# Hybrid SSD / S5 / Conformer step on one core: where the SSD output is split, where state work is queued, and how the LayerNorm mean is made

## The chip, the cores and the metric

One core of a Trainium2 chip runs the whole program. The metric is the device time of one launch in microseconds (us); the kernel before takes 1678.6 us, the median of three runs (1676.21 to 1682.48).

## What is computed

Two layers run for a prompt group of 512 tokens and a sample group of 8 x 8 tokens that share all weights; both groups lie side by side as 576 columns, and the 1024 channels are eight tiles of 128 partitions.

```python
# layer 0
xn = rms_norm(x)
proj = xn @ w_in                       # z | x,B,C | dt | u
ya = mamba2(proj[...])                 # 4 groups: y*silu(z), RMSNorm in the group, * norm_w
yb = s5(proj[...])                     # complex diagonal scan, GELU, GLU with w_glu
x = x + concat([ya, yb]) @ w_out
x = x + square(relu(rms_norm(x) @ w_ff1)) @ w_ff2
# layer 1
h = rms_norm(x) @ w_pw1 + b_pw1        # 2048 columns
h = h[:, :1024] * sigmoid(h[:, 1024:])
h, new_buf = causal_depthwise_conv(h, buf, w_dw, b_dw)     # 31 taps for each channel
h = silu(layer_norm(h))                # mean and variance over the 1024 channels
x = x + h @ w_pw2 + b_pw2
x = x + square(relu(rms_norm(x) @ w_ff1)) @ w_ff2
y = rms_norm(x)
```

Beside `y` the new states are outputs: conv buffers, the SSD states (`o_assm`), the S5 states and the depthwise buffers (`o_cconv`).

## The kernel before, in words

Everything is fp32. A matmul of activations and weights is made of three fp32r products (hi·hi, hi·lo, lo·hi). `mm` (L215) does one 128-column block of weights: 8 slices of the contraction x 3 products x 2 halves of 288 columns = 48 matmuls into one PSUM tile. Its weights come through `load` (L203): `raw` by a DMA that SP issues (L208), `hi` by ScalarE (L211), `lo` by VectorE (L212), each in two buffers, so SP, ScalarE and VectorE must each get through one block while TensorE multiplies another.

A scheduler fixes the order on each engine when the program is built; each engine then runs its list in order, and an instruction that waits holds up all behind it. `hp` raises the priority of what is in it; everything else takes the place the scheduler's own estimate gives it, which can be far ahead of where the code stands.

The stages, in us of the profiled span: mixer of layer 0 to about 585 (`mixer0`, the last part of it the w_out product), MLP 0 (`_ffn(0)`) to 1000, Conformer (`conformer`) to 1255, MLP 1 to 1650, final norm to 1672.5. What the change touches:

- **SSD output** (`a_group`, L975 to L988): each of four groups ends with two tiles `ya` scaled by `rg` (L986) and written to DRAM as `yad` (L987). Before the first half of w_out, `reload` (L1120, L1142) reads eight `yad` tiles back (`rl`) and splits them with `split_scaled` into `yah` (ScalarE, L248) and `yal` (VectorE, L249). Each block m of that product reads its `x` from `xrd` (L1146) and adds the PSUM tile to it (L1148).
- **State work** in MLP 0 (`_ffn`, L367 to L377): in each of 8 up/down pairs of q = 0 stands one piece of `ssm_state` (sample update of the SSD state: `bt`, `xw`, `h` in by DMA; `bm`, `xs`, `bs`, `h` on VectorE; `ss` on TensorE, L1022; `o_assm` out, L1025), and in each of q = 1 one piece of `dwconv_state` (`hs` in, `o_cconv` out, products `pr` and sums `ss` on VectorE, L1329 and L1330). They need nothing of the MLP, and the scheduler draws many of them ahead into the w_out stretch.
- **Conformer loop** (L1179 to L1200): two `mm` per m (16 in all), then `hb`, the gated input of the depthwise convolution. A channel tile's 31 taps are done in one of three ways: on TensorE out of order-of-four layouts (`dwconv_pe`, m in `PT`, 36 matmuls `pc<-hq`, L1308), as VectorE multiply-adds (L1376, `ND[m]` of them), or as diagonal fp32r matmuls (`pc<-hh`, L1374, 3 for each tap).
- **LayerNorm**: the mean over channels comes from `tap_sums` (`pt<-hb`, L1259), which is written to DRAM (`pzd`) and read back skewed (`pk`), and from `mu<-pk` (L1282); `nmu` is added to the tiles as they are ready. Squares go to `tsum` (L1216, 80 records), then the reciprocal root, a broadcast (`bc`, `rBl`), the scaling (L1222), Silu (L1223), the split (L256, L258, L259) and the eight blocks of w_pw2 (L1226).

Of the kernel before, what the change touches and what calls it, by code (L numbers as in the profile page):

```python
# [8 lines left out]
F32 = mybir.dt.float32  # L9
# [6 lines left out]
NT = 576  # L16
# [126 lines left out]
class Build:  # L143
# [32 lines left out]
    X2 = 9  # L176
# [24 lines left out]


    def load(self, src, eng=None):  # L203
# [11 lines left out]
    def mm(self, src, act, eng=None, halves=(0, 1)):  # L215
# [5 lines left out]
        for kb in range(8):  # L221
# [104 lines left out]
    def _ffn(self, i, x):  # L326
# [397 lines left out]
    def a_conv_init(self):  # L724
# [15 lines left out]
        self.yad = [self.dp.tile([128, NT], F32, tag="yad%d" % i, name="yad%d" % i) for i in range(8)]  # L740
# [127 lines left out]
    def a_group(self, g, q, X, bank):  # L868
# [174 lines left out]
    def mixer0(self):  # L1043
        nc, I = self.nc, self.I
        with self.tc.tile_pool(name="q1", bufs=5) as self.q1, ExitStack() as inner:
# [43 lines left out]
            q2 = []  # L1089
# [30 lines left out]
            def reload(d, f):  # L1120
                out = []
                for k in range(8):
# [30 lines left out]
    ND = [0, 30, 0, 0, 30, 0, 30, 14]  # L1153

    NEV = 1
    ORD = [0, 1, 2, 3, 4, 5, 6, 7]
# [12 lines left out]
    PT = [0, 2, 3, 5]  # L1169
    NDM = 5  # L1170

    def conformer(self, x):
        nc, I = self.nc, self.I
        with self.tc.tile_pool(name="q2", bufs=2) as q:
# [3 lines left out]
            ps31 = [self.bank("pt0"), self.bank("pt1", "sf")]  # L1178
            for m in range(8):  # L1179
# [3 lines left out]
                nc.scalar.activation(s, s, AF.Sigmoid, bias=self.v("bpw1", 8 + m))  # L1183
                ps = self.mm(I["w_pw1"][m], act)
# [17 lines left out]
            self.dwconv(q, 7, hbs[7], acc[7], nmu)  # L1202
            nmu = nmu[0]

            ts = self.bank("tsum")
            for n, k in enumerate(self.ORD):
                if k < 7:
                    nc.vector.tensor_tensor(acc[k], acc[k], nmu, op=ALU.add)
                s = self.B("sq")
                if self.SQ[n] == "a":  # L1210
                    nc.scalar.activation(s, acc[k], AF.Square)
                else:
                    nc.vector.tensor_tensor(s, acc[k], acc[k], op=ALU.mult)
                for c in (0, 4, 1, 2, 3):
                    m = min(128, NT - c * 128)
                    nc.tensor.matmul(ts[:m, c:c + 1], s[:, c * 128:c * 128 + m], self.ones[:, 0:1], start=n + c == 0, stop=(n, c) == (7, 3))  # L1216
# [3 lines left out]
            act = []  # L1220
            for k in range(8):
                nc.vector.tensor_tensor(acc[k], acc[k], rB, op=ALU.mult)  # L1222
                nc.scalar.activation(acc[k], acc[k], AF.Silu, scale=self.v("lnw", k), bias=self.v("lnb", k))  # L1223
                act.append(self.split(acc[k], "fx", self.B, k == 0))
# [4 lines left out]
    def dwconv_init(self, q):  # L1229
# [7 lines left out]
        self.bdc = q.tile([128, 8], F32, tag="bdc", name="bdc")  # L1237
        self.neg = q.tile([128, 128], F32, tag="neg", name="neg")
        nc.gpsimd.memset(self.neg, -1.0 / 1024)
        self.pzd = self.dp.tile([31, 670], F32, tag="pzd", name="pzd")  # L1240
# [4 lines left out]
    def dwconv_center(self):  # L1245

        nc = self.nc
        s = self.tp.tile([128, NT], F32, tag="sa", name="s1", bufs=1)
        nc.vector.tensor_reduce(s[:, 0:64], self.ss.rearrange("p m t -> p t m"), axis=mybir.AxisListType.X, op=ALU.add)
        nc.vector.tensor_reduce(s[:, 64:65], self.v("bdw", 0, 8), axis=mybir.AxisListType.X, op=ALU.add)  # L1250
        ps = self.bank("cm")
        nc.tensor.matmul(ps[:, 0:65], self.neg, s[:, 0:65], start=True, stop=True)
        nc.vector.tensor_tensor(self.ss, self.ss, ps[:, 0:64].unsqueeze(1).broadcast_to([128, 8, 64]), op=ALU.add)
        nc.vector.tensor_tensor(self.bdc, self.v("bdw", 0, 8), ps[:, 64:65].broadcast_to([128, 8]), op=ALU.add)

    def tap_sums(self, q, m, hb, ps):

        for h in range(2):
            self.nc.tensor.matmul(ps[h][:31, 0:H], self.v("dww", m * 31, 31), hb[:, 30 + h * H:30 + h * H + H], start=m == 0, stop=m == 7)  # L1259

    def neg_mean(self, q, ps):

        nc = self.nc
        pz = q.tile([31, 670], F32, tag="pz", name="pz", bufs=1)
        pk = q.tile([31, NT], F32, tag="pk", name="pk", bufs=1)
        nc.gpsimd.memset(pz[:, 0:30], 0.0)
        nc.gpsimd.memset(pz[:, 542:670], 0.0)
        nc.gpsimd.memset(pk[:, NP:NT], 0.0)
        out = q.tile([128, NT], F32, tag="nmu", name="nmu", bufs=1)
        with self.hp():  # L1270
            nc.scalar.activation(pz[:, 30:30 + H], ps[0][:31, 0:H], AF.Copy)
            nc.scalar.activation(pz[:, 30 + H:542], ps[1][:31, 0:NP - H], AF.Copy)
            nc.scalar.activation(pz[:, 542:670].rearrange("p (b j) -> p b j", b=8)[:, :, 8:16],
                                 ps[1][:31, NP - H:H].rearrange("p (b j) -> p b j", b=8), AF.Copy)
            nc.sync.dma_start(self.pzd, pz)
            nc.scalar.activation(q.tile([31, 1], F32, tag="ld", name="ld", bufs=1), pz[:, 31:32], AF.Silu)
            d = self.pzd
            nc.sync.dma_start(pk[23:31, NP:NT], bass.AP(tensor=d.tensor, offset=d.offset + 23 * 671 + 520, ap=[[671, 8], [16, 8], [1, 8]]))
            nc.sync.dma_start(pk[:, 0:NP], bass.AP(tensor=d.tensor, offset=d.offset, ap=[[671, 31], [1, NP]]))
            mu = self.pm.tile([128, 2, 512], F32, tag="mm", name="mu")[:, :, :H]  # L1280
            for h, o, n in ((0, 0, H), (1, 0, NP - H), (1, NP - H, 64)):
                nc.tensor.matmul(mu[:, h, o:o + n], self.neg[:31], pk[:, h * H + o:h * H + o + n], start=True, stop=True)  # L1282
            nc.scalar.activation(h2(out), mu, AF.Copy)
        return out, pk
# [7 lines left out]
    def dwconv_pe(self, q, m, hb, a):  # L1292
# [18 lines left out]
        with self.hp(self.HPC):  # L1311
# [5 lines left out]
            nc.scalar.activation(a[:, 0:NP].rearrange("p (n f) -> p f n", f=4), y, AF.Identity, bias=self.bdc[:, m:m + 1])  # L1317
# [15 lines left out]
    def dwconv(self, q, m, hb, a, nmu=None):  # L1333
# [9 lines left out]
        if nmu is not None:  # L1343
            nc.vector.tensor_tensor(a[:, NP:], a[:, NP:], nmu[0][:, NP:], op=ALU.add)
# [7 lines left out]
        nc.scalar.activation(ap, hb[:, 0:NP], AF.Identity, scale=w(0), bias=self.bdc[:, m:m + 1])  # L1352
        pc = None
        if k0 < 31:
# [6 lines left out]
            if nmu is not None:  # L1361
                with self.hp(self.HPC):
                    nc.tensor.matmul(pc, self.neg[:31], nmu[1][:, 0:NP], start=True, stop=False)
            for k in range(k0, 31, 4):
# [7 lines left out]
                for j in range(n):  # L1372
                    for i, (dd, h) in enumerate(((dh, hh), (dh, hl), (dl, hh))):
                        nc.tensor.matmul(pc, dd[:, j], h[:, k + j:k + j + NP], start=k + j == k0 and i == 0 and nmu is None, stop=k + j == 30 and i == 2)  # L1374
        for k in range(1, k0):
            nc.vector.scalar_tensor_tensor(ap, hb[:, k:k + NP], w(k), ap, op0=ALU.mult, op1=ALU.add)  # L1376
        if pc is None and nmu is not None:
            nc.vector.tensor_tensor(ap, ap, nmu[0][:, 0:NP], op=ALU.add)
# [40 lines left out]
```

## Time and profile before

| | us |
|---|---|
| three runs, median (lowest, highest) | 1678.6 (1676.21, 1682.48) |
| the profiled execution, its own time | 1674.24 |
| its span | 1672.5 |
| TensorE busy (share of the span) | 1591.3 (95%) |
| VectorE busy | 1054.5 (63%) |
| ScalarE busy | 634.8 (38%) |
| granted TensorE clock, mean | 0.97 of full |

All sums are made within the profiled execution, whose time is 4.4 us under the median. An engine's rows give the start, the busy time and the count of merged records; a matmul of 288 columns is one record, an fp32 one that isn't fp32r is two. In the views of waits and of the timeline "<-" names what ended the idle time.

### The profile page before, as it was taken

What the parts mean: (1) busy time and instruction counts of PE and PEld (TensorE: products, weight loads), DVE (VectorE), ACT (ScalarE), POOL (GpSimd) and SP (SyncE); (2) the same over time, 40 slices, a digit from 0 to 9 for tenths busy, and PEclk for the clock granted to TensorE, in tenths of its full rate; (3) what the DMA queues carried; (4) which work ended last, traced back from release to release, by engine and by line L of the source; (5) the groups of instructions that cost most, each with busy time, mean ns of one, the idle gap of its engine ahead of it and who ended that gap; (6) DMA issues with size and microseconds to landing.
All of it is one profiled execution on the core that took longest, in us unless ns stands there. A gap on an engine that the chain in (4) does not pass through costs nothing.

```text
span 1672.5 us, 28815 instructions
## 1 busy us (share of the span) xinstructions
PE 1591.3 (95%) x11833; PEld 1557.6 (93%) x11833; DVE 1054.5 (63%) x1796; ACT 634.8 (38%) x1081; POOL 4.7 (0%) x45
## 2 busy tenths in 40 slices
PE   7999889999998999999999999996799999999997
PEld 7999789989897999999999999995799999999996
DVE  7988899876647966754443557587454443444466
ACT  4244556675514333322222353223333222222244
POOL 0000000000000000000000000000000000000000
PEclk9999999999998999999999999997799999999998
DMA  6644457687766434432222245641022222222234
GB/s 197 180 109 132 131 172 197 197 267 220 251 234 188 94 97 129 154 127 78 87 77 88 78 146 148 189 107 30 25 77 77 89 76 89 85 81 88 78 127 132
DMA packets 149883, 214.43 MB, mean 128 GB/s; under 512 B 59034, under 2 KB 94874, under 8 KB 149752
## 3 DMA queue, kind: packets, MB, share of 16 engines
q1 hardware_dynamic: 146088, 211.28, 41.2%
q8 instruction: 93, 1.52, 0.4%
q10 hardware_dynamic: 3664, 1.32, 0.3%
q14 instruction: 38, 0.31, 0.1%
HBM read 181.22 MB, written 31.34 MB: 127 GB/s over the span
## 4 chain that ended last, share of the span: by engine, by line
PE 82%; DVE 7%; DMA 6%; ACT 2%; issue 1%; SPq 1%; ACTq 0%; DVEq 0%
PE mm L226 72%; PE pc L1308 2%; DVE lo L212 1%; DMA sg<-cumd 1%; DMA rl<-yad 1%; PE pc L1374 1%; PE tsum L1216 1%; PE bc L310 1%; DMA rl<-ybd 1%; DMA rl<-yg 1%; PE pt L1259 1%; DMA ud<-u 1%; PE s5s L600 1%; PE s5y L704 0%; PE s5y L705 0%
## 5 line engine op out<-in xcount | busy, mean ns | idle before, releaser
L211 ACT ACTIVATE hi<-raw 128x1024 fp32r<-128x1024 f32 x217 | 229.7, 1060 | 740.2 <-PE mm L226 685.6
L226 PE MATMUL mm<-fxh,hi 128*128 128x288 f32 x1920 | 418.2, 299 | 23.8 <-ACT hi L211 10.4
L212 DVE TENSOR_TENSOR lo<-raw,hi 128x1024 fp32r<-128x1024 f32 x217 | 264.8, 1221 | 259.0 <-ACT hi L211 257.5
L226 PE MATMUL mm<-fxh,lo 128*128 128x288 f32 x1920 | 417.4, 298 | 0.0
L226 PE MATMUL mm<-fxl,hi 128*128 128x288 f32 x1920 | 415.0, 298 | 0.0
L226 PEld LDWEIGHTS mm<-fxh,hi 128*128 128x128 f32 x1920 | 311.7, 190 | 26.7 <-ACT hi L211 12.7
L226 PEld LDWEIGHTS mm<-fxh,lo 128*128 128x128 f32 x1920 | 311.6, 190 | 1.8 <-issue 1.1
L226 PEld LDWEIGHTS mm<-fxl,hi 128*128 128x128 f32 x1920 | 311.9, 190 | 0.4
L226 PE MATMUL mm<-gh,hi 128*128 128x288 f32 x1024 | 230.0, 295 | 0.0
L226 PE MATMUL mm<-gh,lo 128*128 128x288 f32 x1024 | 229.4, 295 | 0.5 <-DVE lo L212 0.5
L226 PE MATMUL mm<-gl,hi 128*128 128x288 f32 x1024 | 229.5, 295 | 0.0
L226 PEld LDWEIGHTS mm<-gh,lo 128*128 128x128 f32 x1024 | 167.5, 188 | 0.8 <-DVE lo L212 0.8
L226 PEld LDWEIGHTS mm<-gl,hi 128*128 128x128 f32 x1024 | 167.9, 188 | 0.0
L226 PEld LDWEIGHTS mm<-gh,hi 128*128 128x128 f32 x1024 | 167.6, 188 | 0.0
L350 DVE TENSOR_TENSOR fft<-mm,r2B 128x576 f32<-128x576 f32 x56 | 42.4, 758 | 140.5 <-PE mm L226 140.5
L1376 DVE SCALAR_TENSOR_TENSOR acc<-hb,vec,acc 128x512 f32<-128x512 f32 x104 | 77.2, 748 | 1.3
L343 DVE TENSOR_TENSOR ffr<-ffr 128x576 f32<-128x576 f32 x64 | 48.5, 758 | 2.3 <-ACT gh L342 0.4
L344 DVE TENSOR_TENSOR gl<-ffr,gh 128x576 fp32r<-128x576 f32 x64 | 48.5, 758 | 2.1
L342 ACT ACTIVATE gh<-ffr 128x576 fp32r<-128x576 f32 x64 | 44.1, 689 | 2.0
L351 DVE TENSOR_TENSOR x<-x,fft 128x576 f32<-128x576 f32 x56 | 42.4, 758 | 1.8
L765 DVE SCALAR_TENSOR_TENSOR cvo<-xb,vh,cvo 128x600 f32<-128x600 f32 x48 | 40.0, 833 | 1.4 <-ACT cvo L763 1.4
L340 ACT ACTIVATE ffr<-mm 128x576 f32<-128x576 f32 x64 | 40.6, 634 | 0.0
(356 smaller groups left out, 1903.1 us busy)
## 6 DMA issues: line engine op xcount, KB each, us to landing
raw<-w_ff SPq DMA_DIRECT2D x136, 512.0 KB, 3.5
raw<-w_in SPq DMA_DIRECT2D x33, 512.0 KB, 3.7
raw<-w_pw SPq DMA_DIRECT2D x24, 512.0 KB, 3.6
dm<-dwm SPq DMA_DIRECT2D x16, 576.0 KB, 5.9
h<-ass SPq DMA_DIRECT2D x16, 512.0 KB, 4.7
raw<-w_out SPq DMA_DIRECT2D x16, 512.0 KB, 4.5
U<-ud SPq DMA_DIRECT2D x16, 288.0 KB, 3.0
xsd<-xs SPq DMA_DIRECT2D x16, 288.0 KB, 4.0
```

Of the source, the lines that this page charges most:

```text
L211: nc.scalar.activation(hi, raw, AF.Copy)
L212: eng.tensor_tensor(lo, raw, hi.bitcast(F32), op=ALU.subtract)
L226: nc.tensor.matmul(ps[:, h, :H], w[:, k], a[:, h * H:(h + 1) * H], start=n == 0, stop=n == 23)
L340: nc.scalar.activation(h2(r), ps, AF.Relu)
L342: nc.scalar.activation(hi, r, AF.Square)
L343: nc.vector.tensor_tensor(r, r, r, op=ALU.mult)
L344: nc.vector.tensor_tensor(lo, r, hi.bitcast(F32), op=ALU.subtract)
L350: nc.vector.tensor_tensor(h2(t), ps, rB, op=ALU.mult)
L351: nc.vector.tensor_tensor(x[m], x[m], t, op=ALU.add)
L765: nc.vector.scalar_tensor_tensor(o[:, 0:600], xb[:, k:k + 600], self.half("acw", 16 * k + m), o[:, 0:600], op0=ALU.mult, op1=ALU.add)
L1308: nc.tensor.matmul(pc[:, g * 128:g * 128 + 128], w[:, j * 128:j * 128 + 128], hq[:, g, j:j + 128], start=j == 0, stop=j == 8)
L1376: nc.vector.scalar_tensor_tensor(ap, hb[:, k:k + NP], w(k), ap, op0=ALU.mult, op1=ALU.add)
```

## The change

1. The two `ya` tiles of groups 1 to 3 are split where they lie, as soon as `rg` is applied, into twelve tiles `yx`; only group 0 goes through DRAM. The w_out product takes the slices in the order 2 to 7, 0, 1. The pool in which `yx` lies gives one buffer (`X2` 9 to 8).
2. `behind_load` lets the pieces of state work issue only after the three instructions of the weight load before them. `dwconv_center` is gone.
3. The mean comes from 16 fp32 matmuls `mu<-acc` that add up in two PSUM banks as the tiles get ready; `tap_sums` and `neg_mean` are gone. `PT` and `ND` are others. After the mean come eight adds on VectorE, squares on ScalarE, four sums of two squares on VectorE, and half as many `tsum` matmuls. `chain` fixes the order on VectorE and ScalarE.

```diff
@@ load @@
-            nc.sync.dma_start(raw, src)
-            nc.scalar.activation(hi, raw, AF.Copy)
-            eng.tensor_tensor(lo, raw, hi.bitcast(F32), op=ALU.subtract)
+            self.last = [nc.sync.dma_start(raw, src), nc.scalar.activation(hi, raw, AF.Copy),
+                         eng.tensor_tensor(lo, raw, hi.bitcast(F32), op=ALU.subtract)]
@@ new @@
+    def chain(self, ins):
+        for a, b in zip(ins, ins[1:]):
+            self.tc.add_manual_dep(b.ins, a.ins.name, mybir.DependencyInfo(mybir.DependencyClass.NoSync, mybir.DependencyReason.DATA),
+                                   reason="chain")
+    def behind_load(self):
+        with ExitStack() as st:
+            for i in self.last:
+                st.enter_context(self.tc.issue_after(i.ins))
+            yield
@@ _ffn @@
                 if q == 1 and i == 0:
-                    self.dwconv_state(self.qp, m)
-                    if m == 7:
-                        self.dwconv_center()
+                    with self.behind_load():
+                        self.dwconv_state(self.qp, m)
                 if q == 0 and i == 0:
-                    self.ssm_state(self.qp, m)
+                    with self.behind_load():
+                        self.ssm_state(self.qp, m)
@@ a_group @@
             nc.vector.tensor_tensor(ya[j], ya[j], rB, op=ALU.mult)
-            nc.sync.dma_start(self.yad[2 * g + j], ya[j])
+            if g:
+                self.ya[2 * g + j] = self.split_scaled(ya[j], self.v("anorm", 2 * g + j), "ya",
+                                                       lambda n, dt: self.yp[0].tile([128, NT], dt, tag="yx", name=n, bufs=12))
+            else:
+                nc.sync.dma_start(self.yad[j], ya[j])
@@ mixer0 @@
+            act += [self.ya[k] for k in range(2, 8)]
...
-                ps = self.mm(I["w_out"][m], act)
+                ps = self.mm(I["w_out"][m], act, order=(2, 3, 4, 5, 6, 7, 0, 1))
@@ conformer @@
-    ND = [0, 30, 0, 0, 30, 0, 30, 14]
+    ND = [0, 30, 0, 30, 0, 30, 0, 20]
-    PT = [0, 2, 3, 5]
+    PT = [0, 2, 4, 6]
...
-                with self.hp(self.HP if m == 7 else 0):
-                    self.tap_sums(q, m, hb, ps31)
                 if m > 0:
                     self.dwconv(q, m - 1, hbs[m - 1], acc[m - 1])
-            nmu = self.neg_mean(q, ps31)
+                if m > 1 and m - 2 not in self.PT:
+                    self.mean(mu, acc, m - 2, done)
+                if m > 3 and m - 4 in self.PT:
+                    self.mean(mu, acc, m - 4, done)
+            self.dwconv(q, 7, hbs[7], acc[7])
+            for m in self.ORD:
+                if m not in done:
+                    self.mean(mu, acc, m, done)
+            for h in range(2):
+                nc.scalar.activation(nmu[:, h * H:h * H + H], mu[h][:, 0:H], AF.Copy)
...
+            for n, k in enumerate(self.ORD):
+                dve.append(nc.vector.tensor_tensor(acc[k], acc[k], nmu, op=ALU.add))
+                sq.append(self.B("sq"))
+                nc.scalar.activation(sq[n], acc[k], AF.Square)
+                if n in (2, 4, 6):
+                    pair(n - 2)
+            pair(6)
+            self.chain(dve)
...
+            for k in range(9):
+                if k < 8:
+                    dve.append(nc.vector.tensor_tensor(acc[k], acc[k], rB, op=ALU.mult))
+                    sca.append(nc.scalar.activation(acc[k], acc[k], AF.Silu, scale=self.v("lnw", k), bias=self.v("lnb", k)))
+                    act.append((self.B("fxh", F32R), self.B("fxl", F32R)))
+                    sca.append(nc.scalar.activation(act[k][0], acc[k], AF.Copy))
+                if k:
+                    dve.append(nc.vector.tensor_tensor(act[k - 1][1], acc[k - 1], act[k - 1][0].bitcast(F32), op=ALU.subtract))
+            self.chain(dve)
+            self.chain(sca)
@@ mean @@
+        for h in range(2):
+            self.nc.tensor.matmul(mu[h][:, 0:H], self.neg, acc[m][:, h * H:h * H + H], start=not done, stop=len(done) == 7)
```

Three places show how the instructions move. First SP's list around the reloads of the SSD output; `raw<-w_out` are the weights of the w_out product, `xr` and `xrd` its x. Before:

```order
L1124 DMA rl<-yad_413 128x576
L1146 DMA x_6506<-xrd_352 128x576
L1003 DMA h_7305<-ass 128x1024
L1323 DMA hs<-ccs 128x8x30
L999 DMA bt_7589<-btd_396 64x128
L1124 DMA rl<-yad_414 128x576
L1139 DMA xrd_353<-xr 128x576
L208 DMA raw<-w_out 128x1024
L1124 DMA rl<-yad_415 128x576
L1324 DMA o_cconv<-hs 128x8x22
L1000 DMA xw_7590<-xwd_400 64x256
L1124 DMA rl<-yad_416 128x576
```

And with the change, from the first reload on:

```order
L1142 DMA rl<-yad_411 128x576
L1165 DMA x_6424<-xrd_351 128x576
L1157 DMA xrd_352<-xr 128x576
L1142 DMA rl<-yad_412 128x576
L224 DMA raw<-w_out 128x1024
L1165 DMA x_6482<-xrd_352 128x576
L1157 DMA xrd_353<-xr 128x576
L224 DMA raw<-w_out 128x1024
L1165 DMA x_6540<-xrd_353 128x576
L224 DMA raw<-w_out 128x1024 x4
L224 DMA raw<-w_ff_0 128x1024 x9
```

Eight reloads are two, and no `h`, `hs`, `bt`, `xw`, `o_cconv` stands among the weights of w_out any more; the first of them come behind nine blocks of MLP 0.

Second, TensorE at the end of the Conformer loop; `mm<-fxh` is the last block of w_pw1. Before:

```order
L226 MATMUL mm<-fxh,lo 128x288 x2
L1259 MATMUL pt_10964<-hb,vec 31x288
L1259 MATMUL pt_10965<-hb,vec 31x288
L1282 MATMUL mu<-pk,neg 128x288
L1282 MATMUL mu<-pk,neg 128x224
L1282 MATMUL mu<-pk,neg 128x64
L1363 MATMUL pc<-pk,neg 128x512
L1374 MATMUL pc<-hh,dh 128x512
```

With the change:

```order
L239 MATMUL mm<-fxh,lo 128x288 x2
L1310 MATMUL pc<-hq,dm 128x128 x36
L1285 MATMUL mu_10931<-acc,neg 128x288
L1285 MATMUL mu_10932<-acc,neg 128x288
L1371 MATMUL pc<-hh,dh 128x512
L1371 MATMUL pc<-hl,dh 128x512
L1371 MATMUL pc<-hh,dl 128x512
```

The skewed reload is gone from the way to the mean; the last `pc<-hq` (m = 6) has moved behind the last block, and three pairs `mu<-acc` stand behind the 30 `pc<-hh`.

Third, VectorE in MLP 0 at the first pair of q = 0; `ffr` and `gl` belong to the up block before, `lo` to the weights. With the change:

```order
L225 TENSOR_TENSOR lo<-raw,hi 128x1024
L1024 TENSOR_TENSOR bm<-bt_7275,cst 32x512
L1035 TENSOR_TENSOR h_7279<-h_7279,cds 128x1024
L1033 TENSOR_TENSOR xs<-xw_7276,xs 32x256
L356 TENSOR_TENSOR ffr<-ffr 128x576
L1029 TENSOR_TENSOR bs<-bm,bs 32x512
L357 TENSOR_TENSOR gl<-ffr,gh 128x576
L225 TENSOR_TENSOR lo<-raw,hi 128x1024
L356 TENSOR_TENSOR ffr<-ffr 128x576
L357 TENSOR_TENSOR gl<-ffr,gh 128x576
L1041 TENSOR_TENSOR h_7279<-h_7279,ss 128x512 x2
L225 TENSOR_TENSOR lo<-raw,hi 128x1024
```

The first piece, which before stood in the w_out stretch, now stands here, and its last step stands in front of a `lo`.

## Rows read from the trace of the kernel before

**Rows 1.** The page, part 4: shares of the chain that ended last, by engine.

```profile
PE 82%; DVE 7%; DMA 6%; ACT 2%; issue 1%; SPq 1%; ACTq 0%; DVEq 0%
```

**Rows 2.** Waits of PE over the span: us in total, times, longest.

```profile
PE mu L1282 <- DMA pk<-pzd: 10.7, 1, 10.7
...
PE mm L226 <- DVE fxh L256: 6.2, 1, 6.2
...
PE mm L226 <- ACT yah L248: 2.6, 3, 1.2
...
PE mm L226 <- DVE yal L249: 2.4, 2, 2.1
```

**Rows 3.** Busy time by stretch: PE, PEld, DVE, ACT, POOL, clock, DMA share, GB/s.

```profile
506.94:585.38 78.44, 70.10 (x479) 67.51 (x477) 69.89 (x83) 29.50 (x40) 0.93 (x6) 0.93 0.58 142
...
535.00:600.00 65.00, 65.00 (x478) 64.78 (x477) 60.16 (x79) 21.94 (x28) 0.93 (x6) 0.98 0.49 110
650.00:727.00 77.00, 77.00 (x583) 77.00 (x582) 53.69 (x69) 29.87 (x44) 0.00 (x0) 1.00 0.48 157
...
1000.00:1135.20 135.20, 135.20 (x1024) 128.59 (x1023) 102.28 (x187) 38.81 (x44) 0.42 (x4) 1.00 0.49 142
...
1135.20:1192.80 57.60, 34.95 (x151) 28.37 (x150) 34.40 (x69) 18.85 (x34) 0.00 (x0) 0.65 0.05 14
```

**Rows 4.** Chain of waits, 490 to 700: start, us, what.

```profile
518.48 5.73 DMA o_assm<-h
...
646.93 0.47 PE ss L1022 x4
647.40 12.78 PE mm L226 x96
```

**Rows 5.** Timeline of PE in the w_out product: start, us, what.

```profile
521.80 0.69 PE L226 MATMUL mm<-yah,hi 128*128 128x288 f32 x2
```

**Rows 6.** Timeline of DVE behind groups 0 and 1.

```profile
429.67 1.23 DVE L212 TENSOR_TENSOR lo<-raw,hi 128x1024 fp32r<-128x1024 f32 x1 [4.35 <-ACT hi L211]
```

**Rows 7.** Groups of PE in the Conformer loop, 1000 to 1135.2: busy, mean ns | idle.

```profile
L1308 PE MATMUL pc<-hq,dm 128*128 128x128 f32 x288 | 33.6, 276 | 0.0
L1259 PE MATMUL pt<-hb,vec 128*31 128x288 f32 x28 | 8.1, 411 | 0.0
```

**Rows 8.** Group of DVE in the same stretch: the multiply-adds.

```profile
L1376 DVE SCALAR_TENSOR_TENSOR acc<-hb,vec,acc 128x512 f32<-128x512 f32 x80 | 59.9, 748 | 1.2
```

**Rows 9.** Chain of waits, 1120 to 1260.

```profile
1138.62 1.84 PE pt L1259 x4
...
1140.96 5.51 DMA pzd<-pz
...
1146.83 4.21 DMA pk<-pzd
...
1168.58 13.03 PE tsum L1216 x80
...
1186.97 5.44 DVE acc L1222 x8
...
1192.83 61.51 PE mm L226 x446
```

**Rows 10.** Timeline of DVE behind the last block of w_pw1.

```profile
1137.76 0.81 DVE L1189 SCALAR_TENSOR_TENSOR hb<-ct,vec,cs 128x576 f32<-128x576 f32 x1
...
1155.07 3.43 DVE L1208 TENSOR_TENSOR acc<-acc,nmu 128x576 f32<-128x576 f32 x5
...
1162.68 4.68 DVE L1376 SCALAR_TENSOR_TENSOR acc<-hb,vec,acc 128x512 f32<-128x512 f32 x6
```

**Rows 11.** Timeline of ACT in the same stretch.

```profile
1153.57 0.65 ACT L1283 ACTIVATE nmu<-mu 128x576 f32<-128x576 f32 x1 [11.11 <-PE mu L1282]
...
1187.76 6.18 ACT L1223 ACTIVATE acc<-acc,vec 128x576 f32<-128x576 f32 x8 [0.83 <-DVE acc L1222]
1193.85 2.39 ACT L258 ACTIVATE fxh<-acc 128x576 fp32r<-128x576 f32 x4
```

More of the change, by code (lines that the diff above doesn't have):

```diff
@@ L1 @@
-from contextlib import ExitStack
+from contextlib import ExitStack, contextmanager
 import numpy as np
@@ L175 @@
     GL = 4
-    X2 = 9
+    X2 = 8
     HPS = 54
@@ L220, in mm @@
         n = 0
-        for kb in range(8):
+        for kb in order:
             ah, al = act[kb]
@@ L739, in a_conv_init @@
         self.ybd = [self.dp.tile([128, NT], F32, tag="ybd%d" % i, name="ybd%d" % i) for i in range(8)]
-        self.yad = [self.dp.tile([128, NT], F32, tag="yad%d" % i, name="yad%d" % i) for i in range(8)]
+        self.yad = [self.dp.tile([128, NT], F32, tag="yad%d" % i, name="yad%d" % i) for i in range(2)]
     def half(self, n, i=0):
@@ L1088, in mixer0 @@
             ssd = [[], []]
-            q2 = []
+            q2 = self.yp = []
+            self.ya = {}
             def side(na):
@@ L1121, in reload @@
                 out = []
-                for k in range(8):
+                for k in range(len(d)):
                     t = self.t("rl", "t")
@@ L1183, in conformer @@
                 nc.scalar.activation(s, s, AF.Sigmoid, bias=self.v("bpw1", 8 + m))
+                if m == 7:
+                    nc.scalar.activation(q.tile([128, 1], F32, tag="ld", name="ld", bufs=1), s[:, 0:1], AF.Silu)
                 ps = self.mm(I["w_pw1"][m], act)
@@ L1196, in conformer, with pair @@
                         self.dwconv_mat(q, m, g)
-                with self.hp(self.HP if m == 7 else 0):
-                    self.tap_sums(q, m, hb, ps31)
                 if m > 0:
                     self.dwconv(q, m - 1, hbs[m - 1], acc[m - 1])
-            nmu = self.neg_mean(q, ps31)
-            self.dwconv(q, 7, hbs[7], acc[7], nmu)
-            nmu = nmu[0]
-            ts = self.bank("tsum")
[L1206 to L1213, printed above, removed]
+                if m > 1 and m - 2 not in self.PT:
[6 more added lines that the diff above has]
+                    self.mean(mu, acc, m, done)
+            nmu = q.tile([128, NT], F32, tag="nmu", name="nmu", bufs=1)
+            for h in range(2):
+                nc.scalar.activation(nmu[:, h * H:h * H + H], mu[h][:, 0:H], AF.Copy)
+            ts = self.bank("tsum")
+            dve, sq = [], []
+            def pair(n):
+                dve.append(nc.vector.tensor_tensor(sq[n], sq[n], sq[n + 1], op=ALU.add))
                 for c in (0, 4, 1, 2, 3):
                     m = min(128, NT - c * 128)
-                    nc.tensor.matmul(ts[:m, c:c + 1], s[:, c * 128:c * 128 + m], self.ones[:, 0:1], start=n + c == 0, stop=(n, c) == (7, 3))
+                    nc.tensor.matmul(ts[:m, c:c + 1], sq[n][:, c * 128:c * 128 + m], self.ones[:, 0:1], start=n + c == 0, stop=(n, c) == (6, 3))
+            for n, k in enumerate(self.ORD):
[6 more added lines that the diff above has]
+            self.chain(dve)
             r = self.tp.tile([128, 5], F32, tag="r5", name="r5")
@@ L1219, in conformer @@
             rB = self.bcast_tok(r, "rBl")
[L1220 to L1224, printed above, removed]
+            act, dve, sca = [], [], []
+            for k in range(9):
[8 more added lines that the diff above has]
+            self.chain(sca)
             for m in range(8):
@@ L1243, in dwconv_init @@
         self.dm = {}
[L1245 to L1254, printed above, removed]
@@ L1256, in tap_sums @@
-    def tap_sums(self, q, m, hb, ps):
-        for h in range(2):
[L1259 to L1284, printed above, removed]
@@ L1286, in dwconv_mat, with mean @@
+    def mean(self, mu, acc, m, done):
+        for h in range(2):
+            self.nc.tensor.matmul(mu[h][:, 0:H], self.neg, acc[m][:, h * H:h * H + H], start=not done, stop=len(done) == 7)
+        done.append(m)
     def dwconv_mat(self, q, m, g):
@@ L1360, in dwconv @@
             pc = self.bank("pc", "sd" if m % 2 else "sf")
-            if nmu is not None:
-                with self.hp(self.HPC):
-                    nc.tensor.matmul(pc, self.neg[:31], nmu[1][:, 0:NP], start=True, stop=False)
             for k in range(k0, 31, 4):
@@ L1373, in dwconv @@
                     for i, (dd, h) in enumerate(((dh, hh), (dh, hl), (dl, hh))):
-                        nc.tensor.matmul(pc, dd[:, j], h[:, k + j:k + j + NP], start=k + j == k0 and i == 0 and nmu is None, stop=k + j == 30 and i == 2)
+                        nc.tensor.matmul(pc, dd[:, j], h[:, k + j:k + j + NP], start=k + j == k0 and i == 0, stop=k + j == 30 and i == 2)
         for k in range(1, k0):
             nc.vector.scalar_tensor_tensor(ap, hb[:, k:k + NP], w(k), ap, op0=ALU.mult, op1=ALU.add)
-        if pc is None and nmu is not None:
-            nc.vector.tensor_tensor(ap, ap, nmu[0][:, 0:NP], op=ALU.add)
         if pc is not None:
```

18 lines of the change are left out of this document (8 added, 10 removed).

## The prediction

> **What bounds the kernel now.** First the chain that ended last: 82% of it is TensorE [rows 1], so time is won only where TensorE stands still or runs at its lower clock, and where other work is taken off it. Then TensorE's waits: the two long ones that the change touches are at the LayerNorm, 10.7 us for the reloaded `pk` and 6.2 us for the first split; the splits of the SSD output cost 5.0 [rows 2]. Then the stretches: from 1135.2 to 1192.8 TensorE is busy 34.95 of 57.60 us at 0.65 of its clock; from 506.94 to 585.38, the w_out product and its tail, 70.10 of 78.44 at 0.93; the Conformer loop is full, 135.20 of 135.20; so are two stretches that hold state work, 65.00 of 65 and 77.00 of 77 [rows 3]. So three places can give time: w_out, where waits and clock count; the loop, where only TensorE's own work counts; and the LayerNorm, a single chain of steps.
>
> **The change, part by part.**
>
> *w_out.* The price of a matmul of 288 columns is 12.78/96 = 0.133 us at 2.4 GHz [rows 4]. From 506.94 to 585.38 stand 12 + 372 matmuls of the product, 86 of the next stage (the order's count) and one `ss` of 0.47 us [rows 4]. 470 x 0.133 = 62.6, so 15.9 us are lost there: waits for the splits, 5.0 [rows 2]; for `ss` and the sums behind state work; and clock, since behind the waits a pair takes 0.48 us from start to start (0.69 busy) [rows 5] in place of 0.27. The chain runs here through `o_assm<-h` [rows 4], nothing that the product needs. With the change six of eight slices are split long before (groups 1 and 2 in a VectorE gap of 4.35 us [rows 6], group 3 about ten us ahead), the other two come last in the order, state pieces are gone, and the 384 matmuls stand in a row. I take all but the `ss`, which is issued later: **-15.4**. Bounds: -15.9, and -5 if only the named waits of [rows 2] go. I take the upper one because nothing that stalled there is left in front of it. The saved transfers (six writes, six reloads) were in SP's list beside TensorE work: 0, at most 1 either way; one buffer fewer in the pool of groups 1 and 3: 0, at worst +2, covered by the gap of [rows 6].
>
> *State work in MLP 0.* Sixteen pieces now stand in sixteen up/down pairs of 12.78 us [rows 4], behind the weight loads. TensorE's part (4 short matmuls for a piece) is the same, only later: +0.5, already in the line above. VectorE's and SP's parts count only where they hold up `lo` or `raw`. Before, six SSD pieces ran in the same manner in 650 to 727 and TensorE was full, VectorE 53.69 of 77; with conv pieces VectorE was at 60.16 of 65 and TensorE still full [rows 3]. **0**; if the cover goes, see the first rival. `dwconv_center` was hidden: 0.
>
> *Conformer loop.* TensorE bounds it, so its work counts in full. Out: seven `tap_sums`, 8.1 us, and one of four `pc<-hq`, 33.6/4 = 8.4, which goes behind the last block [rows 7]. In: four pairs `mu<-acc` of the same shape in columns as `pt`, 8.1/7 = 1.16 each, 4.6. **-11.9.** VectorE must keep up: 102.28 us busy in 135.20 [rows 3], 80 taps among them [rows 8]; now some 89 of 110 taps fall into the loop, 9 x 0.75 = 6.7 more, in 11.9 less: 109 of 123, 88%. Bounds: -11.9, and 0 if VectorE takes over.
>
> *LayerNorm.* Let E be the end of the last block, 1135.2 before. Before, the first block of w_pw2 starts at 1192.83 [rows 9], E + 57.6. After:
> - `hb` of m = 7 is there at 1137.76 + 0.81 [rows 10], E + 3.4.
> - VectorE then does a tap of m = 5, `hl`, eight small ones and 20 dependent taps: 4.68/6 = 0.78 each [rows 10], 15.6; the others fill the gaps between taps in part and are estimated at three taps, 2.3; the sum with `pc` 0.7. E + 22. This is the step that waits ends on: the moved `pc<-hq` (8.4) and 30 diagonal matmuls lie beside it on TensorE, which is idle by then.
> - Two pairs `mu`, at 1.2 GHz as `pt` at the same place before, 1.84 each [rows 9]: E + 25.7. Two evacuations of half the width for the one of 0.65 [rows 11], 0.8 as an estimate: E + 26.5.
> - On VectorE eight adds and three sums in a fixed order, 3.43/5 = 0.69 each [rows 10], 7.6; then the last square and the last sum, 0.7 each: E + 35.5.
> - The last ten `tsum` records, 13.03/80 = 0.163 each [rows 9], 1.6; to the scaling as before (1181.61, the end of `tsum`, to 1186.97), 5.4; one scaling 5.44/8 [rows 9], one Silu 6.18/8, one split 2.39/4 [rows 11], 2.1: E + 44.6.
>
> The gain is 13.0. From it goes the end of the first two blocks of w_pw2, which run side by side: both evacuations and the next `hi`, `lo` fall into one place, about 1.5 by the same rows (0.75 + 0.75). **-11.5.** Bounds: -14 (`mu` at full clock, no stall) and -5 (each of the 12 fixed steps waits 0.5 for its partner).
>
> The rows price a tap by what dependent ones took, 0.78, and an add of 576 columns at 0.69 [rows 10]. The Trainium skill ("VectorE: DVE Perf Modes", section on the TRN2 errata) gives (N + 151)/0.96 ns for an fp32 add of two tensors. Estimated by that page, 20 taps of 512 columns would take 13.8 and twelve steps of 576 columns 9.1, and the LayerNorm would come out 1 us shorter; the trace disagrees in both places, and the sum goes by the trace.
>
> *Sum.* -15.4 - 11.9 - 11.5 = -38.8. On the profiled execution 1674.24 that is 1635.4; it lies 4.4 under the median 1678.6, so the forecast for a median is **1640**.
>
> **The rivals.**
>
> *Slower: state pieces hold up the weights.* Place: the sixteen pairs of MLP 0. `h<-h,ss` or `pr` waits on VectorE for a transfer or for `ss`, `lo` stands behind it, and SP's `raw` behind `o_assm`. It decides when a pair loses more than 38.8/16 = 2.4 us. At 3 us a pair the cost is 48, and the time 1640 + 48 = 1688. For it: every piece now stands in front of a `lo`, and one `o_assm` took 5.73 on the chain [rows 4]. Against: [rows 3], six such pieces with TensorE at 77.00 of 77. Chance 4%; a partial one of 1 us a pair gives 1656, the end of the range.
>
> *VectorE becomes the bound of the Conformer.* At 88% in the loop, with taps in front of `lo` in a fixed list, half-microsecond waits become TensorE's. Then the loop gains nothing and the time is 1640 + 11.9 = 1652. For it: the last stretch before was already near it. Against: the mean of 88%, and every `lo` has a block's time. Chance 16%. The Trainium skill ("VectorE: DVE Perf Modes", Rules for kernel authors) says to keep the number of VectorE operations down, which speaks against a change that adds six taps and four sums; the trace agrees as far as dependent taps cost 0.78 each.
>
> *The w_out product still waits.* The change then doesn't do there what it says: the first slices or the weights come late for another reason (SP's writes of `xrd` in front of `raw`, the evacuation with `x`). Half of the 15.4 stays lost: 1648. For it: more than half of what is lost there is not in the named waits. Against: [rows 6] and the shorter SP list. Chance 10%.
>
> *The two blocks side by side run at 1.2 GHz.* Each slice then waits for its producers, and the clock that fell in the LayerNorm (0.65 [rows 3]) does not come back until they end: 96 x 0.133 = 12.8 more, less the 61.51 - 446 x 0.133 = 2.1 that the start at the lower clock costs today [rows 9]: 1640 + 10.7 = 1651. For it: in w_out TensorE ran at 1.2 GHz just behind such waits [rows 5]. Against: a slice needs 12 x 0.133 = 1.6 us of TensorE, ScalarE makes one in 0.77 + 0.60 and VectorE in 0.68 + 0.7 [rows 9, 11]. Chance 8%. The Trainium skill ("TensorE: Matmul & The Clock Gate", HAM oscillation) describes such a loop, short work and a wait in each step of the contraction, as one that starts every step cold; whether it applies hangs on the wait, which these rows don't give.
>
> **How the numbers follow.** The forecast has 57%, the four rivals 4, 16, 10 and 8, and 5 is left for a gain larger than summed (the bounds -15.9 and -14, and relief in the SSD stretch: 1634 and below). The 0.5% that a measurement of this kernel can tell from no change is 8.4 us, or 1670.2. Three milder rivals alone leave the time at 1648 to 1652, faster; two together reach 1663; only all three (1640 + 30.3 = 1670) or the first rival end within or beyond the bound. Faster 0.93, same 0.04, slower 0.03. The range: below, the upper bounds of all three terms (0.5 + 2.5) and three us of spread of the runs, with some for the SSD stretch, 1630; above, one rival with the same spread, 1656.
>
> **What would show it.** w_out: no wait of TensorE on `yah`, `yal` or `x`, its 384 matmuls in 51 us at clock 1.00. MLP 0: TensorE full in every pair; a wait on `lo` or `ss` there is the first rival. Loop: the last block of w_pw1 ends 27 us earlier than now (15.4 + 11.9); if later, the wait on `lo` names the second. LayerNorm: 45 us from there to the first block of w_pw2, with `mu` waiting for `acc` of m = 7 and `tsum` for the last sum; the two blocks at clock 1.00 soon after their start. The prediction is wrong if MLP 0 grows, or if the three places together give less than 22.

## The result and the profile after

| | before, us | after, us |
|---|---|---|
| median of four runs (lowest, highest) | 1680.5 (1676.2, 1683.6) | 1637.3 (1636.4, 1643.8) |
| the same once more, nine and five runs | 1676.3 (1673.6, 1677.5) | 1642.1 (1636.1, 1648.9) |
| profiled execution, its span | 1674.24, 1672.5 | 1643.81, 1641.8 |

The ratio is 0.9745 with a 95% interval of 0.9715 to 0.9775, and 0.9802 (0.9776 to 0.9829) the second time: 43 and 34 us. The forecast was 1640 (1630 to 1656) against 1678.6. The profile was taken of the slowest of the first four runs, so its spans differ by 30.7 only; why, the first experiment tells.

The chain that ended last has more of TensorE and less of transfers than [rows 1] (page, part 4):

```profile
PE 85%; DVE 7%; DMA 4%; ACT 1%; issue 1%; SPq 1%; ACTq 0%; DVEq 0%
```

Busy time by stretch, columns as in [rows 3]: the w_out product and the work behind it, MLP 0, the Conformer loop, the LayerNorm, and the first two blocks of w_pw2:

```profile
513.30:571.17 57.87, 57.87 (x438) 57.87 (x436) 28.55 (x34) 20.27 (x26) 0.15 (x1) 1.00 0.29 98
571.17:1000.00 428.83, 428.83 (x3224) 428.58 (x3223) 254.28 (x326) 143.64 (x202) 1.57 (x15) 1.00 0.39 113
1000.00:1114.00 114.00, 113.28 (x875) 112.05 (x875) 102.36 (x179) 35.13 (x40) 0.41 (x4) 1.00 0.53 151
1114.00:1160.24 46.24, 32.83 (x170) 28.36 (x168) 32.93 (x64) 12.82 (x20) 0.00 (x0) 0.72 0.12 33
1160.24:1178.00 17.76, 17.07 (x106) 16.41 (x107) 13.04 (x18) 13.63 (x19) 0.00 (x0) 0.86 0.00 1
```

The reader is to see three things. TensorE has no idle time and its full clock from 513.30 on through MLP 0, where VectorE now holds all the state work and still has 41% free. In the loop VectorE is at 102.36 of 114.00, 90%, and TensorE at 99%. The LayerNorm is 46.2 us for 57.6 in [rows 3], still with a lowered clock.

The four longest waits of TensorE that are left from 505 to 1200, in us, times, longest (the two others are 0.7 and 0.5). Of those in [rows 2] only the one for the first split of w_pw2 is left, 2.7 for 6.2, now for ScalarE:

```profile
PE mu L1285 <- DVE acc L1375: 4.7, 1, 4.7
PE tsum L1240 <- DVE sq L1237: 3.5, 1, 3.5
PE mm L239 <- ACT fxh L1259: 2.7, 1, 2.7
PE bc L323 <- DVE rv L302: 2.5, 1, 2.5
```

And the chain of waits through the LayerNorm, which answers to [rows 9]:

```profile
1135.12 0.70 DVE acc L1375
1135.86 4.22 PE mu L1285 x8
1140.10 0.42 ACT nmu L1231
...
1143.54 8.86 PE tsum L1240 x40
...
1154.86 2.06 PE bc L323 x8
...
1160.24 14.76 PE mm L239 x92
...
1177.76 45.83 PE mm L239 x342
```

No transfer stands between the taps and the mean any more. Behind the two blocks of w_pw2, which run side by side, the chain leaves TensorE until 1177.76 for evacuations (`x`) and `lo` of the third block; TensorE itself is idle for 0.7 of these 2.7 us and does a few matmuls in the rest.

Where the 30.7 us of the two profiles came from, by instants read off the groups of `mm` by what they multiply and off the chain (the last w_pw1 block counts as ended when its last matmul hands over to the next, 0.2 us ahead of the end that [rows 3] uses):

| stretch | before | after | forecast | measured |
|---|---|---|---|---|
| start of the span to the first matmul of w_out with `yah` | 506.9 | 513.3 | 0 | +6.4 |
| to the first matmul of MLP 0's down part | 127.1 | 111.9 | -15.4 | -15.2 |
| to the end of the last w_pw1 block | 501.0 | 488.8 | -11.9 | -12.2 |
| to the first w_pw2 matmul | 57.8 | 46.2 | -13.0 | -11.6 |
| to the end of the span | 479.7 | 481.6 | +1.5 | +1.9 |

### The profile page after: what moved, and what is told of

Same layout as the page of the kernel before. It is cut to its first block, busy times and chain, and to the rows that moved or that the text cites. A ratio compares the mean times of both kernels' runs of the same rounds, so it can differ in the third digit from the quotient of the medians.

```text
span 1641.8 us, 28632 instructions
## 1 busy us (share of the span) xinstructions
PE 1577.4 (96%) x11765; PEld 1551.6 (95%) x11765; DVE 1058.1 (64%) x1801; ACT 631.2 (38%) x1068; POOL 4.3 (0%) x42
## 4 chain that ended last, share of the span: by engine, by line
PE 85%; DVE 7%; DMA 4%; ACT 1%; issue 1%; SPq 1%; ACTq 0%; DVEq 0%
PE mm L239 76%; PE pc L1310 1%; DVE lo L225 1%; PE yoff L979 1%; DVE acc L1373 1%; PE s5y L717 1%; PE bc L323 1%; PE s5y L718 1%; DMA sg<-cumd 1%; DMA ud<-u 1%; DMA eb<-ecd 1%; PE tsum L1240 1%; PE yps L937 0%; PE mu L1285 0%; SPq L592 0%
## 5 line engine op out<-in xcount | busy, mean ns | idle before, releaser
L1373 DVE SCALAR_TENSOR_TENSOR acc<-hb,vec,acc 128x512 f32<-128x512 f32 x110 | 82.6, 751 | 1.5
```

## The experiments

Times are compared in two ways. The median against the kernel before on the same chip is one. The other is T, the time in a profile from the first matmul of the w_out product with `yah` to the end of the span: 1165.6 before and 1128.5 after. There is one kept profile of each kernel below, so a T has no interval of its own, and four of the runs (the second one of before, the doubled state pieces, 18 and 14 taps) are single executions.

**Both kernels once more.** No edit.

> The changed kernel once more, unaltered, as the measure for the three beside it on the same chip and as a second profile. Theory: from the first matmul of the w_out product to the end it takes 1128.5 us as in the first profile, within 1; what the two profiles differ by lies ahead of it, where the start of that product moved between 506.9 and 513.3 us from profile to profile of kernels that share all work up to there. Rival (the changed pool or the earlier splits cost 6 us ahead of w_out): it starts at 513 us again.

> The kernel before, unaltered, for a second profile. Theory: the start of the w_out product moves by some us from execution to execution (506.9 in the first profile, 512.7 and 513.1 in two kernels with the same order up to there), while from there to the end it takes 1165.6 us as in the first, but for the round trip of the mean through DRAM (5.5 + 4.2 us there), which may differ by 2 us or so. Rival: the stretch ahead of w_out is fixed for a kernel, and starts w_out at 507 again.

The product started at 510.9 and 510.3, and T was 1639.4 - 510.9 = 1128.5 and 1676.0 - 510.3 = 1165.7, to 0.1 us as in the first profiles. These are the instants: tile `yah`, PE, of the second profile of before, and of two kernels below whose lists are those of before up to the last transfers ahead of this product (the tie alone, and the mean alone):

```profile
L226 PE MATMUL mm<-yah,hi x128: 290/295/606, 510.3 to 575.8; 128*128 128x288 f32 x128
```

```profile
L234 PE MATMUL mm<-yah,hi x128: 292/295/608, 512.7 to 569.6; 128*128 128x288 f32 x128
```

```profile
L239 PE MATMUL mm<-yah,hi x128: 288/292/608, 513.1 to 578.3; 128*128 128x288 f32 x128
```

Over fourteen profiles of all kernels it lay between 506.6 and 513.3. So the start moves by 6 us among kernels with the same lists ahead of it (by 3.4 and 2.4 between the two profiles of an unaltered one), the first profile of before had one of the earliest starts, and the +6.4 can't be put down to the change. The difference comes in several steps: the second profile of before is 0.6 early after 1350 matmuls of the program, 4.8 late after 2550 and 3.4 late at the product.

T repeats better, but not always to 0.1 us. In the kernel before the parts of T differ by up to 0.6 between the two profiles and happen to cancel, and in the next two experiments below, which share its LayerNorm, that stage took 59.6 and 60.6 us for 57.8. Between the two pairs of profiles the change gains 1165.6 - 1128.5 = 37.1 us; against a LayerNorm as slow as the slowest it would be 40. The medians' 43 and 34 lie around both. The spans of nine executions of the changed kernel reach from 1634.3 to 1647.1, more than the start's 6.7; where the rest of that lies no kept profile shows.

**Only the split in place**, on the kernel before:

```diff
-            nc.sync.dma_start(self.yad[2 * g + j], ya[j])
+            if g:
+                self.ya[2 * g + j] = self.split_scaled(...)
+            else:
+                nc.sync.dma_start(self.yad[j], ya[j])
...
-                ps = self.mm(I["w_out"][m], act)
+                ps = self.mm(I["w_out"][m], act, order=(2, 3, 4, 5, 6, 7, 0, 1))
```

> The kernel before with only the split in place (six tiles split where they lie, order 2 to 7, 0, 1, one pool buffer fewer). The 384 matmuls of the w_out product then stand in a row, but the conv pieces of the state work still stand among the weights of the last blocks and of MLP 0. Theory (late splits are most of the loss): 10 to 15 us faster than before, w_out product of 51 to 56 us instead of 66.5. Rival (state work in front of the weight loads is the loss): under 8 us faster, with waits on lo or x in the product. Conformer unchanged, 57.6 us from its last w_pw1 block to the first w_pw2 block.

1664.9 us, ratio 0.9916 (0.9887 to 0.9945): 15.0 faster than the median of before, 1679.9. The product takes 51 us; the stretch from it, busy times as above:

```profile
508.80:575.00 66.20, 66.20 (x500) 66.17 (x499) 39.48 (x53) 25.34 (x34) 0.31 (x2) 1.00 0.36 110
```

TensorE is full, so no loss is left in the product, though nothing ties the state work here: with the slices ready, the scheduler itself issues the first state transfer at 558.6, at the product's end, and the state pieces that were expected among its weights are not there. The split, the order of the slices and the smaller pool came in together; no run parts these three.

T is 1153.2, 12.4 less, and the median shows 15.0; 2.8 of the stage's 15.2 were lost behind it, 1.8 of them in the LayerNorm, where 59.6 us passed from the last w_pw1 block to the first of w_pw2. The edit doesn't touch that code, but the order on ScalarE came out another way: a table load (L1282) now stands ahead of two of the three copies into `pz` (L1278, L1279), which in the kernel before came ahead of it.

```profile
1127.25 1.28 ACT L1282
...
1128.98 0.12 ACT pz L1279
1129.12 5.53 DMA pzd<-pz
...
1134.99 4.77 DMA pk<-pzd
```

So the wait for `pk` was 13.1 where [rows 2] had 10.7, while the two transfers took 10.3 for the 9.7 of [rows 9].

**Only the tie behind the weight loads**, on the kernel before:

```diff
-                    self.ssm_state(self.qp, m)
+                    with self.behind_load():
+                        self.ssm_state(self.qp, m)
```

and the same for `dwconv_state`.

> The kernel before with only the state work tied behind the weight loads; all eight tiles of the SSD output still go through DRAM. Theory (late splits): eight reloads through three buffers at 5.7 us each stay behind the first block, so waits on yah and yal of 4 to 8 us stay and the kernel is only 7 to 11 us faster. Rival (state work): the reloads were late only because state transfers stood among them, and all 15 us are gained. MLP 0 stays full in both; if it does not, the state pieces cost there what they cost in w_out.

1671.3 us, ratio 0.9942 (0.9923 to 0.9960), T 1159.2: 8.6 and 6.4 us, the latter with a LayerNorm that took 60.6 us for 57.8. There the wait for `pk` was 10.6, as before; what took longer is TensorE's work, at a lower granted clock: `tsum` 15.1 us at 0.56 for 13.0 at 0.67, `pc` 13.9 at 0.80 for 13.2 at 0.84. The product shrank from 66.5 to 57.4; waits on `yah` of 2.5 us stay, less than the 4 to 8 expected, and the chain shows what from (start, us, what):

```profile
514.14 3.17 DMA xrd<-xr
517.30 0.02 issue
517.32 3.84 DMA rl<-yad
521.16 0.02 issue
521.19 0.78 ACT yah L256
521.97 0.03 issue
522.00 0.83 DVE yal L257
522.82 0.04 issue
522.87 7.05 PE mm L234 x38
```

A write of `xrd` stands ahead of a reload in SP's list, and the split behind it. So of the 15.5 us that the product loses, 6.4 (57.4 less 51.0) stay with the late splits when the state pieces are gone; the split in place takes all of it.

**The change without the tie.**

```diff
-                    with self.behind_load():
-                        self.ssm_state(self.qp, m)
+                    self.ssm_state(self.qp, m)
```

> The changed kernel without the tie of the state work to the weight loads (dwconv_center stays out). Theory: with the tiles split in place the scheduler leaves the w_out product whole anyway, and the tie adds nothing: within 2 us of the changed kernel. Rival (the three parts add up as their single gains do, 15.0 + 8.6 + 21.9): the tie still gives 5 us or more, so this kernel is slower by that.

1642.5 against 1642.1 of the changed kernel beside it; T 1638.6 - 510.2 = 1128.4. The tie adds nothing that these runs can tell once the tiles are split in place. The single gains don't add up because two of them are the same microseconds. The whole without the split, with the tie left in, was not run.

**Only the mean, the taps and the fixed orders** (the first two parts undone in the changed kernel).

> The changed kernel with its first two parts undone: only the mean in PSUM, the other split of taps and the fixed orders. Theory (sum of terms): 23.4 us faster than before (loop 11.9, LayerNorm 11.5), w_out product as before at 66.5 us. Rival (VectorE becomes the bound in the loop): under 14 us faster.

1657.9 us, ratio 0.9871 (0.9845 to 0.9898): 21.9; T 1142.7: 22.9. With the 15.2 that the split brings in its own stage that is 38.1 for the 37.1 of all; with its T, which has the slower LayerNorm in it, 12.4 + 22.9 = 35.3.

**No fixed order.**

```diff
-        for a, b in zip(ins, ins[1:]):
+        for a, b in ():
```

> The changed kernel without the fixed order on VectorE and ScalarE: the list then has all eight adds before the four sums of squares, and all eight scalings before the eight second splits. Theory: the first tsum starts 5 x 0.7 = 3.5 us later and the first split of w_pw2 6 x 0.7 = 4.2 later, so 5 to 8 us slower than the changed kernel (about 1644). Rival (order does not matter, since tsum at the lower clock or ScalarE sets the pace): within 2 us of it.

1648.1 us, ratio 0.9817 (0.9789 to 0.9844), T 1133.5: 5.0 slower than the changed kernel by T, at the lower end of what was expected; the ratios, 0.9817 against 0.9745 and 0.9802, put it anywhere from 2 to 12. The chain:

```profile
1140.06 4.76 DVE acc L1243 x7
1144.82 0.68 DVE sq L1237
...
1145.54 8.57 PE tsum L1240 x40
...
1159.54 5.44 DVE acc L1256 x8
1164.98 0.68 DVE fxl L1261
...
1165.70 14.35 PE mm L239 x88
```

The timeline of PE has the start of w_pw2 (start, us, what, [idle before]):

```profile
1162.58 1.33 PE L239 MATMUL mm<-fxh,hi 128*128 128x288 f32 x4 [3.34 <-ACT fxh L1259]
1165.70 0.85 PE L239 MATMUL mm<-fxl,hi 128*128 128x288 f32 x2 [1.79 <-DVE fxl L1261]
```

Eight adds before the first sum put `tsum` 6.6 us behind the start of `nmu`, where it is 3.4 in the changed kernel. Eight scalings before the first second half of a split (`fxl`) let TensorE do four matmuls at 1162.58, then wait; it goes on at 1165.70, 9.1 behind `bc`, where the changed kernel starts 5.4 behind it. Of these 6.9 us about 2 come back: the four matmuls are done, and the end of the two blocks loses nothing here (the 25 matmuls from the 96th on take 3.3 us, in the changed kernel 4.8).

**The taps of before, the mean in PSUM.**

```diff
-    ND = [0, 30, 0, 30, 0, 30, 0, 20]
-    PT = [0, 2, 4, 6]
+    ND = [0, 30, 0, 0, 30, 0, 30, 14]
+    PT = [0, 2, 3, 5]
```

> The changed kernel with the split of the taps of the kernel before (PT 0, 2, 3, 5; ND 30, 30, 30, 14), the mean still in PSUM. Theory: the last w_pw1 block ends 8.4 us later, since one pc<-hq stands in the loop again, but behind it VectorE has six taps fewer of tile 7 and tile 6's left over, and one mean pair more waits at the end; so 4 to 8 us slower than the changed kernel. Rival (TensorE does not bound the loop): the end of the last block moves by under 3 us.

1648.5 against 1642.1, T 1136.8, 8.3 slower. From w_out to the end of the last w_pw1 block 610.5 us passed for 600.7: one `pc<-hq` (8.0) and one more mean pair (1.0) stand in the loop. TensorE bounds the loop, and the moved matmuls are worth about what they last. Behind the loop 1.5 us come back by T; the medians show 6.4 in all.

**State pieces made twice**, the output being the same:

```diff
-        for i in range(2):
+        for i in (0, 1, 0, 1):
```

> The changed kernel with the products and sums of each conv piece made twice, 4.6 us more of VectorE in each of the eight pairs of q = 1 (the output is the same). It asks how far the cover in MLP 0 goes. Theory: a pair has 12.78 us and VectorE then needs about 15, but the list lets the pieces fall behind into later pairs, whose VectorE is half idle, so TensorE stays full: under 2 us from the first matmul of w_out to the end. Rival (pieces stand in front of lo, and each pair is lengthened): 2.2 x 8 = 17 us.

T 1635.6 - 508.3 = 1127.3. In the part of MLP 0 where the doubled pieces lie:

```profile
730.00:870.00 140.00, 140.00 (x1052) 140.00 (x1051) 118.82 (x131) 36.84 (x44) 0.92 (x6) 1.00 0.36 93
```

VectorE went from 87.77 in the same stretch of the changed kernel to 118.82 of 140, 85%, and TensorE stayed full. T is 1.2 less than the changed kernel's, though there is more to do: its two last mean pairs ran at a higher clock (see the next experiment). For the conv pieces the cover is more than twice what the change uses; the SSD pieces were not doubled.

**Fewer taps on VectorE for tile 7**, `ND[7]` 18, 16 and 14 for 20.

> The changed kernel with 18 taps of tile 7 on VectorE. Theory: the gain from 20 to 16 taps has two parts, 0.78 us for each tap and about 2 us for mean pairs at full clock once TensorE's idle time ahead of them is short. At 18 taps the idle time is still about 2 us, so the first part alone gives 1127; with the clock kept, 1125.

> The changed kernel with 16 taps of channel tile 7 on VectorE for 20, four more on TensorE (12 matmuls of 0.23 us). Theory: the LayerNorm waits for VectorE's taps, TensorE is idle for 4.7 us ahead of the last two mean pairs, so the mean starts 2 to 3 us earlier, and with the shorter idle time TensorE may keep its clock there, for 2 us more: 2 to 5 us faster than the changed kernel. Rival (the diagonal weights that ScalarE builds are late, since a fourth tile needs a buffer to come free): no gain or a loss.

> The changed kernel with 14 taps of tile 7 on VectorE. Theory: at 16 taps TensorE already runs without a wait from the last w_pw1 block to the last mean pair, so six more diagonal matmuls cost 1.4 us: 1126 us from the first matmul of w_out to the end, against 1124.7 at 16 taps and 1128.5 at 20. Rival (VectorE still sets the pace at 16): 1123.

T was 1124.9, 1124.7 and 1125.1, against 1128.5 at 20. Sixteen taps took 1638.2 us, ratio 0.9773 (0.9755 to 0.9791), beside 1642.1 and 0.9802 (0.9776 to 0.9829) of the changed kernel; by the profile that is the fastest version here, by 3.8 us, which those two intervals don't yet part. By T two taps fewer gain 3.6, more than the 1.6 that they last: 18 taps gave the 1125 expected with the clock kept, not the 1127 without. The timeline of PE at 20 taps and at 18 shows the rest (start, us, what, [idle before]):

```profile
1135.86 4.21 PE L1285 MATMUL mu<-acc,neg 128*128 128x288 f32 x8 [4.74 <-DVE acc L1375]
1143.54 8.84 PE L1240 MATMUL tsum<-ones,sq 128*128 128x1 f32 x40 [3.47 <-DVE sq L1237]
```

```profile
1132.34 2.21 PE L1285 MATMUL mu<-acc,neg 128*128 128x288 f32 x8 [1.79 <-DVE acc L1375]
1138.02 1.96 PE L1240 MATMUL tsum<-ones,sq 128*128 128x1 f32 x10 [3.47 <-DVE sq L1237]
1140.19 6.66 PE L1240 MATMUL tsum<-ones,sq 128*128 128x1 f32 x30 [0.21 <-DVE sq L1237]
```

And the stretches of the mean pairs and of `tsum` at 20 taps, and of the mean pairs at 18, columns as in [rows 3] (the clock is the third number from the end):

```profile
1135.86:1140.10 4.24, 4.21 (x8) 2.52 (x8) 0.00 (x0) 0.41 (x1) 0.00 (x0) 0.50 0.00 0
1143.54:1152.40 8.86, 8.84 (x40) 8.54 (x40) 5.56 (x8) 3.39 (x5) 0.00 (x0) 0.50 0.00 0
```

```profile
1132.34:1134.55 2.21, 2.21 (x8) 1.43 (x8) 0.00 (x0) 0.41 (x1) 0.00 (x0) 1.00 0.00 0
```

After 4.74 us of waiting the two mean pairs ran at 1.2 GHz (granted 0.50), 0.53 us a record; after 1.79 at 2.4 GHz (1.00), 0.28. That is 2.0 us, and with the two taps' 1.6 it makes the 3.6. At 14 and 16 taps TensorE has no wait left there. From 16 to 14 the way from the last w_pw1 block to w_pw2 grew from 42.1 to 43.5, the 1.4 that was expected of six more matmuls; T shows 0.4, since the loop ahead of it came out 0.8 shorter.

The wait alone does not settle the clock. In the run with the taps of before the last two mean pairs waited 2.29 us and yet ran at 0.57, in the run with doubled state pieces 4.12 and ran at 0.68; and `pt`, which waits 3.4 us for `hb` in all kernels with the mean of before, ran at 0.60 in the first profile of before, at 0.50 in the second and at 1.00 with only the split in place:

```profile
1141.16 3.83 PE L1285 MATMUL mu<-acc,neg 128*128 128x288 f32 x8 [2.29 <-DVE acc L1375]
```

```profile
1130.86 3.12 PE L1285 MATMUL mu<-acc,neg 128*128 128x288 f32 x8 [4.12 <-DVE acc L1375]
```

```profile
1138.62 1.82 PE L1259 MATMUL pt<-hb,vec 128*31 128x288 f32 x4 [3.41 <-DVE hb L1189]
```

```profile
1125.60 1.16 PE L1265 MATMUL pt<-hb,vec 128*31 128x288 f32 x4 [3.43 <-DVE hb L1195]
```

## Why the prediction was right, point by point

- **w_out, -15.4 as forecast, -15.2 measured.** The whole product, no wait on `yah`, `yal` or `x`, 51 us at clock 1.00. The working put the loss down to splits, state work and clock together; the runs part them: the split (with the slice order) alone brings it all, the tie alone 9.1 us of the product. That the tie is not needed the prediction did not see: it took the removal of state pieces as the second part's doing, and the scheduler does it by itself once the slices are early.
- **State work, 0.** TensorE is full in all of MLP 0, and with the conv pieces made twice too. The rival on the slower side fell with a wide margin.
- **Loop, -11.9, measured -12.2.** TensorE bounded it before and after; VectorE came out at 90% where 88% was worked out. The rival of VectorE as the bound fell: the largest wait in the loop is 0.7 us. The rule of the Trainium skill ("VectorE: DVE Perf Modes", Rules for kernel authors) to keep the number of operations down did bite, but behind the loop: there two taps fewer gave 3.6 us of T. The split of the taps is worth the 9.8 us by which the loop's end moves without it, 8.3 in T; what the mean in PSUM and the halved `tsum` bring, without the taps and the fixed order, no run shows alone.
- **LayerNorm, -13.0, measured -11.6.** The steps, from the end of the last block, forecast and measured: `pc` added 22 and 21.9; mean pairs done 25.7 and 26.1; last sum of squares 35.5 and 36.1; `tsum` done 37.1 and 38.4; first split 44.6 and 46.2. So it came out 1.6 late in all, and the largest part of it is the tail of `tsum`, 2.3 for 1.6: 0.163 us a record from [rows 9] is a mean at a clock of 0.67, and here all forty ran at 0.50, 8.86/40 = 0.22. The mean pairs give 0.5: 1.84 was taken as the price at 1.2 GHz, but those records of `pt` ran at 0.60, and at 0.50 two pairs took 4.22. The other 0.4 lie in the adds and sums and between `tsum` and the split. The trace's price of a dependent tap held: 14 took 10.98, 0.78 each. The Trainium skill's formula ("VectorE: DVE Perf Modes", section on the TRN2 errata) is for an fp32 add of two tensors, and of such adds it is right here: it gives 0.69 and 0.76 for 512 and 576 columns, and single adds took 0.69 (`acc<-acc,pc`) and 0.757 (the mean of 56 `x<-x,fft`). The prediction's 0.69 for 576 columns is not the time of one add but the distance from one to the next in a row, so that its "the trace disagrees in both places" was a wrong comparison there; the taps, which are multiply-adds, each on the result of the one before, are no such adds.
- **The two blocks side by side, +1.5, measured +1.9.** Up to the 95th matmul 0.4 us more passed than before, and the end of the two blocks cost the other 1.4 or so, close to the 1.5 put on it. They started at 1.2 GHz and were at 2.4 GHz 5 us later, clock 0.86 over the 17.8 us; the rival in which they stay slow fell. "TensorE: Matmul & The Clock Gate" in the Trainium skill (HAM oscillation) describes a loop that waits in each step; here the list shows a wait ahead of the first slice only, so it doesn't apply. Without the fixed order the clock comes back too, though later: 0.50 until 5.4 us behind the wait for `fxl`, then 1.00.
- **The sum, -38.8, measured -37.1 in T.** The step from the profiled execution to a median, +4.4, is worth no more than the spread of the stretch ahead of w_out. That 1640 lies within 3 us of both medians, 1637.3 and 1642.1, is partly luck, since executions of the one kernel lie 13 us apart; the stages, not the median, bear the working out.

## What to carry to other kernels

Price a change stage by stage between instants that all versions share: here a stretch that the change doesn't touch moves by 6 us, while T repeated to 0.1 in two pairs of profiles and moved by 1 to 3 where the clock or a scheduler's order came out another way. When two parts of a change cure the same wait, test each alone and the whole without each: the gains of the two (15 and 9 us in w_out) overlapped wholly. Where one engine's last few operations decide when another resumes, moving two of them can pay more than they last, where the other engine keeps its clock over the shorter wait: 3.6 us for 1.6 here, though other short waits in these runs ended at the lower clock.

## What the runs showed that was not expected

The start of w_out lay anywhere from 506.9 to 513.1 us in four profiles with the lists of before ahead of it, and from 506.6 to 513.3 with those of the changed kernel. TensorE waited 10.7, 10.9, 10.6 and 13.1 us for `pk` in the four profiles with the mean of before, but the round trip through DRAM itself took 9.7, 9.9, 9.6 and 10.3; the odd one out comes mostly from ScalarE's order. The clock behind waits of 2 to 4 us was no fixed price either: mean pairs of eight records took 4.2, 3.1, 3.8 and 2.2 us after idle times of 4.7, 4.1, 2.3 and 1.8. What makes the mixer's first part move, and what decides the clock behind such waits, was not tried and stays open.
